# A decoder layer on one core: which pairs of a block product use seven products, and when their weight sums and snapshots are made

## The chip, the cores and the metric

The kernel runs on one core of a Trainium2 chip. The metric is device time in microseconds of one execution, given as the median of several runs. Beside the runs there is one profiled execution, from which the views of the trace come. The engines are called PE (matmul), PEld (its weight load), DVE (VectorE), ACT (ScalarE), POOL (GpSimd) and SP (SyncE, which issues the DMAs here).

## The reference

One layer over 16 meta tokens and 256 real tokens of width 2048, in float32: a normed input goes through one combined projection, a differential attention group and a gated DeltaNet group, and an output projection with residual. Then comes the part that is changed, a SwiGLU feed-forward block with a hidden width of 5632:

```python
h = h + jnp.concatenate([o_a, o_d], axis=-1) @ w_out[l]
u = rmsnorm(h, ffn_norm_w[l])
h = h + (jax.nn.silu(u @ w_gate[l]) * (u @ w_up[l])) @ w_down[l]
return h[:, LEAD:]
```

## The kernel before

**Precision.** Each float32 operand of a large product is kept as a high part in the PE's reduced format and a low part, the rest. A product is three matmuls: high × high, high × low, low × high. ACT casts the high part of a weight tile (`S.copy` in `split`, L274), the DVE subtracts it from the raw tile for the low part (L275).

**Weights.** SP loads raw tiles of 128 × 2 × 512 floats (L261) in the order in which they are used, into four slots. `split_to` makes "forms" from them, a high and a low tile each, into six buffers: the cast of a form therefore waits until the PE is done with the form six places earlier. In the FFN each block reads its weights by pairs q of two 128-row k tiles; a pair has two raw tiles (in gate and up the *gate* and the *up* tile, in down the tiles of two neighbouring column groups of 512).

**Blocks.** `block` (product line L1386 here) handles two column groups at once for 256 tokens, so that the output is four PSUM banks x (two column groups × two groups of 128 tokens). With pair q the four banks get a 2 × 2 block product: two k tiles against two column groups. A **plain pair** uses the two raw tiles as two forms and takes eight products, 24 matmuls of 128 × 512. A **seven pair** uses the scheme of seven block products: four forms, g and u (the second half only) from the raw tiles, t and s from sums of them, and 21 matmuls. Four of its products go to four side banks y of the other PSUM ring. The sums t and s take four DVE operations on halves (128 × 512): t at L292 and L293, with the u form; s at L298 and L299, with the t form. So a seven pair gives the DVE four half sums, three whole low parts and a half one; a plain pair two whole low parts.

Activations need sums too: `side_forms` (L1314 to L1333) makes them, on the DVE seven operations (one at L1320, one each at L1322 to L1325, L1331, L1332) and two casts on ACT, once for each seven pair of gate and up and of down.

**Order of the FFN.** First chunk 0 in another form (L1201), then ten chunks of `chunk`, each the gate and up columns of 512 hidden units (8 pairs), then down in two halves p = 0, 1 of 22 pairs each. In a chunk the pairs in `SEVEN` are seven pairs, in a half of down those in `DSEVEN`. After the last seven pair of a block, `mid` starts a task (`mid_task` or `down_mid`) that copies y[0] on ACT (the snapshot, L1346 in a chunk), forms sums with y[1] to y[3] on the DVE, and frees the y banks, which are the x banks of the next block. At the end of a chunk `end_task` adds (L1360, L1365, L1367 in the profile), and `to_hT` transposes the hidden activations on the PE (L1279) and splits them (L1295). Hidden chunks 8, 9 and 10 are first held in float32 and split when down begins, in `whole` (L1467); `fetch_x1` brings the residual back.

**What sets the order.** Side work is written as generators. `tasks.step()` is called after each group of products and lets waiting tasks emit instructions; `delay` is the number of steps before a task may start, `urgent` puts it first. ACT and SP run in the order in which the program emits; PE and DVE are reordered by the framework's scheduler.

Of the kernel before, what the change touches and what calls it, by code (L numbers as in the profile page):

```python
# [15 lines left out]
P = 128  # L16
# [18 lines left out]
SEVEN = (2, 5)  # L35
DSEVEN = (5, 7, 9, 11, 13, 15)
# [130 lines left out]
def layer(tc, xT, aw, x, w_in, w_ba, w_out, w_gate, w_up, w_down, cmask, dist, par, out):  # L167
# [110 lines left out]
    def split_to(n, parts=1):  # L278
        while pos[1] < min(n, len(forms)):
            m = pos[1]  # L280
            kind, i = forms[m]
            load_to(i + (1 if kind in "wg" else 2))
            src, a, b = order[i]
            if kind in "wg":
                ready[m] = split(raws[i], m, a, b, parts)
                if kind == "w":
                    raws.pop(i)
                    pos[3] += 1
            elif kind == "u":
                g, u = raws[i], raws[i + 1]  # L290
                sums_["t"] = more[0].tile([P, 2, 512], F32, tag="sum", bufs=2, name=f"t{i}")
                V.tensor_tensor(sums_["t"][:, 0], u[:, 0], g[:, 0], ALU.subtract)  # L292
                V.tensor_tensor(sums_["t"][:, 1], u[:, 1], u[:, 0], ALU.subtract)  # L293
                ready[m] = split(u, m, a, b, rows=slice(1, 2))
            elif kind == "t":
                g, u, t = raws.pop(i), raws.pop(i + 1), sums_["t"]
                sums_["s"] = s = more[0].tile([P, 2, 512], F32, tag="sum", bufs=2, name=f"s{i}")
                V.tensor_tensor(s[:, 0], u[:, 1], t[:, 0], ALU.subtract)  # L298
                V.tensor_tensor(s[:, 1], g[:, 1], s[:, 0], ALU.subtract)  # L299
                pos[3] += 2  # L300
                ready[m] = split(t, m, a, b)
            else:
                ready[m] = split(sums_["s"], m, a, b)
# [1036 lines left out]
    def mid_task(c, y, t):  # L1340

        ring = rings[(c + 1) % 2]
        for _ in range(4):
            t.append((yield from fpool[1].get(512)))
        s1, w12, u3, w22 = t
        S.copy(s1, y[0])  # L1346
# [70 lines left out]
    def chunk(c):  # L1417
# [7 lines left out]
        block(c, "u", KT // 2, SEVEN, lhs_u, None, lambda y: tasks.spawn(mid_task(c, y, t), urgent=True), end)  # L1425
# [70 lines left out]
    def down_mid(p, y):  # L1496
        yield at_least("x1n", p + 1)
        ring = rings[(NCH + p + 1) % 2]
        s1 = yield from fpool[1].get(512)
        u2 = yield from fpool[1].get(512)  # L1500
        u3 = yield from fpool[1].get(512)
        S.copy(s1, y[0])
        yield 1
# [21 lines left out]
    def down_side(i, q):  # L1525
# [12 lines left out]
        h = hT[q // 2]  # L1538
        yield from side_forms(("h", q), h[:, 0, k, :], h[:, 1, k, :], sh, sl)

    for c in range(WHOLE, NCH):
        tasks.spawn(whole(c), delay=8)
    for i, q in enumerate(DSEVEN):
        tasks.spawn(down_side(i, q), delay=4)
# [77 lines left out]
```

## Time and profile before

| what | us |
|---|---|
| median of 3 runs (lowest to highest) | 1232.11 (1231.4 to 1233.8) |
| profiled execution, its own time | 1230.78 |
| its span, first to last instruction | 1229.0 |
| ten chunks of gate and up, 553.54 to 984.20 | 430.66, PE 429.60, DVE 342.65, ACT 225.06 busy |
| from there to the end (down, output) | 244.80, PE 238.45, DVE 187.71, ACT 117.67 busy |

The busy times of the stretches come from the view of busy time by window. Busy time is a union over an engine's overlapping instructions. The DVE and the PE begin an instruction before the one ahead has ended, so the price of an instruction in a row of such is the distance of two starts, not the length. The chain of waits follows the last instruction back to what released each step; a row of it has start, length, engine, tile and line.

### The profile page before, as it was taken

What the parts mean: (1) busy time and instruction counts of PE and PEld (TensorE: products, weight loads), DVE (VectorE), ACT (ScalarE), POOL (GpSimd) and SP (SyncE); (2) the same over time, 40 slices, a digit from 0 to 9 for tenths busy, and PEclk for the clock granted to TensorE, in tenths of its full rate; (3) what the DMA queues carried; (4) which work ended last, traced back from release to release, by engine and by line L of the source; (5) the groups of instructions that cost most, each with busy time, mean ns of one, the idle gap of its engine ahead of it and who ended that gap; (6) DMA issues with size and microseconds to landing.
All of it is one profiled execution on the core that took longest, in us unless ns stands there. A gap on an engine that the chain in (4) does not pass through costs nothing.

```text
span 1229.0 us, 19155 instructions
## 1 busy us (share of the span) xinstructions
PE 1217.9 (99%) x7352; PEld 1066.9 (87%) x7352; DVE 933.4 (76%) x1487; ACT 672.3 (55%) x1059; POOL 6.0 (0%) x14
## 2 busy tenths in 40 slices
PE   9999999999999999999999999999999999999998
PEld 7999999999999988887888888888888887888887
DVE  7989974686676665667887887888788698876774
ACT  7674465375676655554555545455554555543552
POOL 0000000000000000000000000000000000000000
PEclk9999999999999999999999999999999999999999
DMA  8466553344544645675565656556465655676553
GB/s 293 124 204 196 153 180 118 118 131 147 165 136 149 219 171 178 211 265 169 182 226 160 204 189 218 192 177 229 161 201 191 205 194 182 208 247 232 199 198 117
DMA packets 151867, 228.52 MB, mean 186 GB/s; under 512 B 11736, under 2 KB 72672, under 8 KB 151264
## 3 DMA queue, kind: packets, MB, share of 16 engines
q1 hardware_dynamic: 151232, 226.78, 57.1%
q8 instruction: 57, 0.93, 0.3%
q10 hardware_dynamic: 544, 0.52, 0.1%
q14 instruction: 34, 0.28, 0.1%
HBM read 221.83 MB, written 5.45 MB: 185 GB/s over the span
## 4 chain that ended last, share of the span: by engine, by line
PE 75%; DVE 13%; DMA 6%; ACT 3%; issue 2%; SPq 0%; DVEq 0%; ACTq 0%
PE mm L1154 22%; PE mm L1386 19%; PE aux L1386 17%; PE mm L1201 10%; DVE lo L275 7%; DMA raw<-in_w_down_dram 5%; ACT hi L274 2%; PE aux L1102 1%; DVE t L292 1%; DVE s L298 1%; PE aux L1057 1%; DMA out_dram<-x 0%; DVE s L299 0%; DVE t L293 0%; DMA raw<-in_w_in_dram 0%
## 5 line engine op out<-in xcount | busy, mean ns | idle before, releaser
L275 DVE TENSOR_TENSOR lo<-raw,hi 128x1024 fp32r<-128x1024 f32 (+1 forms) x412 | 475.2, 1170 | 183.6 <-ACT hi L274 178.6
L274 ACT CAST hi<-raw 128x1024 fp32r<-128x1024 f32 (+1 forms) x412 | 410.6, 1008 | 338.9 <-PE mm L1154 92.9
L1154 PE MATMUL mm<-xh,hi 128*128 128x272 f32 (+2 forms) x896 | 258.4, 289 | 0.0
L1154 PE MATMUL mm<-xl,hi 128*128 128x272 f32 (+2 forms) x896 | 255.8, 286 | 0.6 <-DVE xl L386 0.6
L1154 PE MATMUL mm<-xh,lo 128*128 128x272 f32 (+2 forms) x896 | 254.8, 285 | 0.8 <-DVE lo L275 0.8
L1154 PEld LDWEIGHTS mm<-xh,hi 128*128 128x128 f32 x896 | 168.8, 189 | 2.1 <-issue 1.8
L1154 PEld LDWEIGHTS mm<-xl,hi 128*128 128x128 f32 x896 | 168.5, 188 | 1.6 <-DVE xl L386 1.3
L1154 PEld LDWEIGHTS mm<-xh,lo 128*128 128x128 f32 x896 | 168.2, 188 | 1.2 <-DVE lo L275 1.0
L1386 PE MATMUL mm<-hi,uh 128*128 128x512 f32 x280 | 109.4, 391 | 0.0
L1386 PE MATMUL aux<-hi,uh 128*128 128x512 f32 x280 | 109.4, 391 | 0.0
L1386 PE MATMUL aux<-hi,ul 128*128 128x512 f32 x280 | 109.0, 389 | 0.0
L1386 PE MATMUL mm<-hi,ul 128*128 128x512 f32 x280 | 109.0, 389 | 0.0
L1386 PE MATMUL aux<-lo,uh 128*128 128x512 f32 x280 | 109.0, 389 | 0.0
L1386 PE MATMUL mm<-lo,uh 128*128 128x512 f32 x280 | 109.0, 389 | 0.0
L274 ACT CAST hi<-s 128x1024 fp32r<-128x1024 f32 x32 | 33.7, 1052 | 69.4 <-DVE s L299 47.7
L1386 PE MATMUL aux<-hi,hT 128*128 128x512 f32 x208 | 68.4, 390 | 0.0
L1386 PE MATMUL mm<-hi,hT 128*128 128x512 f32 x208 | 68.1, 389 | 0.0
L1386 PEld LDWEIGHTS aux<-hi,ul 128*128 128x128 f32 x280 | 52.6, 188 | 10.9
L1386 PEld LDWEIGHTS mm<-hi,ul 128*128 128x128 f32 x280 | 52.6, 188 | 10.9
L1386 PEld LDWEIGHTS aux<-lo,uh 128*128 128x128 f32 x280 | 52.6, 188 | 10.8
L1386 PEld LDWEIGHTS mm<-hi,uh 128*128 128x128 f32 x280 | 52.6, 188 | 10.8
L1386 PEld LDWEIGHTS aux<-hi,uh 128*128 128x128 f32 x280 | 52.6, 188 | 10.7
(415 smaller groups left out, 1899.9 us busy)
## 6 DMA issues: line engine op xcount, KB each, us to landing
raw<-in_w_in_dram SPq DMA_DIRECT2D x111, 512.0 KB, 3.5
raw<-in_w_gate_dram SPq DMA_DIRECT2D x88, 512.0 KB, 4.3
raw<-in_w_up_dram SPq DMA_DIRECT2D x88, 512.0 KB, 4.5
raw<-in_w_down_dram SPq DMA_DIRECT2D x88, 512.0 KB, 4.5
raw<-in_w_out_dram SPq DMA_DIRECT2D x32, 512.0 KB, 4.3
x<-x1d SPq DMA_DIRECT2D x8, 256.0 KB, 5.4
xr<-in_xT_dram SPq DMA_DIRECT2D x7, 272.0 KB, 5.5
out_dram<-x SPq DMA_DIRECT2D x6, 256.0 KB, 5.6
```

The costliest lines, as they stand in the source:

```text
L274: S.copy(hi[:, js], raw[:, js])
L275: V.tensor_tensor(lo[:, js], raw[:, js], hi[:, js], ALU.subtract)
L292: V.tensor_tensor(sums_["t"][:, 0], u[:, 0], g[:, 0], ALU.subtract)
L298: V.tensor_tensor(s[:, 0], u[:, 1], t[:, 0], ALU.subtract)
L1057: PE.matmul(pss[m][:, cut[n]], q[ms, P * n:P * (n + 1)], k[ms, 0:NK[n]], start=True, stop=True)
L1102: PE.matmul(po[:, n, :], l, r, start=(j == 0), stop=(j == 1 + n))
L1154: PE.matmul(acc[c][:, 0:n], a[:, k, cs], b[:, kt, t0:T], start=(kt == 0 and i == 0), stop=(kt == KT - 1 and i == 2))
L1201: PE.matmul(acc[b], l, r[:, i % 2, :], start=(first and i == 0 and j == 0), stop=(last and i == len(kts) - 1 and j == 2))
L1386: PE.matmul((x if bank[0] == "x" else y)[bank[1]], l, r, start=first, stop=todo[bank] == 0)
```

## The change

`SEVEN` goes from two pairs (2 and 5) to three (2, 4 and 6) of eight, `DSEVEN` from six pairs (5, 7 to 15) to seven (7, 9 to 19) of 22. In `split_to` both sums of weights, t and s, are made in the step of the form g, the pair's first; both raw tiles are let go with u. The snapshot is emitted in `mid` at once, as soon as the tiles for it are free, and the task for the rest starts without delay. The tasks `whole`, `down_side` and `fetch_x1(0)` start after 24 steps instead of 8, 4 and 16, and `down_side` waits for the split of its own hidden chunk.

```diff
@@ -32,8 +32,8 @@
 WR, WS = 4, 4
 WS2 = 2
 WHOLE = 8
-SEVEN = (2, 5)
-DSEVEN = (5, 7, 9, 11, 13, 15)
+SEVEN = (2, 4, 6)
+DSEVEN = (7, 9, 11, 13, 15, 17, 19)
 PER_STEP = 2
 SLOT = 4
 WARM = 14
@@ -279,28 +279,26 @@
         while pos[1] < min(n, len(forms)):
             m = pos[1]
             kind, i = forms[m]
-            load_to(i + (1 if kind in "wg" else 2))
+            load_to(i + (1 if kind == "w" else 2))
             src, a, b = order[i]
-            if kind in "wg":
-                ready[m] = split(raws[i], m, a, b, parts)
-                if kind == "w":
-                    raws.pop(i)
-                    pos[3] += 1
-            elif kind == "u":
+            if kind == "w":
+                ready[m] = split(raws.pop(i), m, a, b, parts)
+                pos[3] += 1
+            elif kind == "g":
                 g, u = raws[i], raws[i + 1]
-                sums_["t"] = more[0].tile([P, 2, 512], F32, tag="sum", bufs=2, name=f"t{i}")
-                V.tensor_tensor(sums_["t"][:, 0], u[:, 0], g[:, 0], ALU.subtract)
-                V.tensor_tensor(sums_["t"][:, 1], u[:, 1], u[:, 0], ALU.subtract)
-                ready[m] = split(u, m, a, b, rows=slice(1, 2))
-            elif kind == "t":
-                g, u, t = raws.pop(i), raws.pop(i + 1), sums_["t"]
-                sums_["s"] = s = more[0].tile([P, 2, 512], F32, tag="sum", bufs=2, name=f"s{i}")
+                ready[m] = split(g, m, a, b)
+                t, s = (more[0].tile([P, 2, 512], F32, tag="sum", bufs=2, name=f"{n}{i}") for n in "ts")
+                V.tensor_tensor(t[:, 0], u[:, 0], g[:, 0], ALU.subtract)
+                V.tensor_tensor(t[:, 1], u[:, 1], u[:, 0], ALU.subtract)
                 V.tensor_tensor(s[:, 0], u[:, 1], t[:, 0], ALU.subtract)
                 V.tensor_tensor(s[:, 1], g[:, 1], s[:, 0], ALU.subtract)
+                sums_["t"], sums_["s"] = t, s
+            elif kind == "u":
+                raws.pop(i)
+                ready[m] = split(raws.pop(i + 1), m, a, b, rows=slice(1, 2))
                 pos[3] += 2
-                ready[m] = split(t, m, a, b)
             else:
-                ready[m] = split(sums_["s"], m, a, b)
+                ready[m] = split(sums_[kind], m, a, b)
             pos[1] += 1
 
     def next_w():
@@ -1340,10 +1338,7 @@
     def mid_task(c, y, t):
 
         ring = rings[(c + 1) % 2]
-        for _ in range(4):
-            t.append((yield from fpool[1].get(512)))
         s1, w12, u3, w22 = t
-        S.copy(s1, y[0])
         yield 1
         V.tensor_tensor(w12, y[1], s1, ALU.add)
         V.tensor_tensor(u3, y[2], w12, ALU.add)
@@ -1422,7 +1417,13 @@
                 for b in range(2):
                     tasks.spawn(end_task(c, b, x, t), urgent=True)
 
-        block(c, "u", KT // 2, SEVEN, lhs_u, None, lambda y: tasks.spawn(mid_task(c, y, t), urgent=True), end)
+        def mid(y):
+            tasks.until(lambda: fpool[1].live == 0)
+            t.extend(fpool[1].now((512,)) for _ in range(4))
+            S.copy(t[0], y[0])
+            tasks.spawn(mid_task(c, y, t), delay=0, urgent=True)
+
+        block(c, "u", KT // 2, SEVEN, lhs_u, None, mid, end)
         mark(f"up{c}")
 
     def keep_x1():
@@ -1493,14 +1494,9 @@
     def need_h(kt):
         return at_least(f"hT{kt // 4}", 2 if kt // 4 < WHOLE else 3)
 
-    def down_mid(p, y):
+    def down_mid(p, y, s1, u2, u3):
         yield at_least("x1n", p + 1)
         ring = rings[(NCH + p + 1) % 2]
-        s1 = yield from fpool[1].get(512)
-        u2 = yield from fpool[1].get(512)
-        u3 = yield from fpool[1].get(512)
-        S.copy(s1, y[0])
-        yield 1
         V.tensor_tensor(u2, y[1], s1, ALU.add)
         V.tensor_tensor(u3, y[2], u2, ALU.add)
         for b, c, t in ((0, 1, y[3]), (1, 1, y[3]), (0, 1, u2), (1, 1, u3), (0, 0, s1), (1, 0, u3)):
@@ -1535,21 +1531,28 @@
                 t = rest[:, o:o + 6 * P]
             sh, sl = (t[:, 3 * P * j:3 * P * (j + 1)].rearrange("p (a b) -> p a b", b=P) for j in range(2))
         k = slice(2 * q % 4, 2 * q % 4 + 2)
-        h = hT[q // 2]
-        yield from side_forms(("h", q), h[:, 0, k, :], h[:, 1, k, :], sh, sl)
+        c = q // 2
+        yield at_least(f"hT{c}", 2 if c < WHOLE else 3)
+        h, l = (hT[c][:, 0], hT[c][:, 1]) if c < WHOLE else hT[c]
+        yield from side_forms(("h", q), h[:, k, :], l[:, k, :], sh, sl)
 
     for c in range(WHOLE, NCH):
-        tasks.spawn(whole(c), delay=8)
+        tasks.spawn(whole(c), delay=24)
     for i, q in enumerate(DSEVEN):
-        tasks.spawn(down_side(i, q), delay=4)
-    tasks.spawn(fetch_x1(0), delay=16)
+        tasks.spawn(down_side(i, q), delay=24)
+    tasks.spawn(fetch_x1(0), delay=24)
     for p in range(2):
         def end(col, x):
             for b in range(2):
                 tasks.spawn(down_end(p, b, col, x[2 * col + b]), urgent=True)
 
-        block(NCH + p, "h", FFN // P // 2, DSEVEN, lhs_h, need_h,
-              lambda y: tasks.spawn(down_mid(p, y), urgent=True), end)
+        def mid(y):
+            tasks.until(lambda: fpool[1].live <= 1)
+            t = [fpool[1].now((512,)) for _ in range(3)]
+            S.copy(t[0], y[0])
+            tasks.spawn(down_mid(p, y, *t), delay=0, urgent=True)
+
+        block(NCH + p, "h", FFN // P // 2, DSEVEN, lhs_h, need_h, mid, end)
         if p == 0:
             tasks.spawn(fetch_x1(1), delay=12)
     tasks.until(lambda: not tasks.list)
```

What the scheduler makes of it is seen in the order of the engines. Place one is the DVE in a steady chunk of gate and up, around a seven pair. Names: `raw` is a loaded tile, `hi` and `lo` a form's parts, `t` and `s` the sums. Before:

```order
L275 TENSOR_TENSOR lo_7593<-raw_7548,hi_7592 128x1024
L275 TENSOR_TENSOR lo_7605<-raw_7575,hi_7604 128x1024
L292 TENSOR_TENSOR t_7614<-raw_7587,raw_7575 128x512
L293 TENSOR_TENSOR t_7614<-raw_7587 128x512
L275 TENSOR_TENSOR lo_7618<-raw_7587,hi_7617 128x512
L298 TENSOR_TENSOR s_7633<-raw_7587,t_7614 128x512
L299 TENSOR_TENSOR s_7633<-raw_7575,s_7633 128x512
L275 TENSOR_TENSOR lo_7637<-t_7614,hi_7636 128x1024
L275 TENSOR_TENSOR lo_7657<-s_7633,hi_7656 128x1024
```

and with the change (pair 4 of a chunk; L291 to L294 are the lines of the four half sums now, and the rows ahead of this piece are two L1293 rows, three whole low parts, one L1362 row and the half low part of the *up* tile of pair 2):

```order
L291 TENSOR_TENSOR t_7622<-raw_7583,raw_7519 128x512
L275 TENSOR_TENSOR lo_7607<-raw_7517,hi_7606 128x1024
L292 TENSOR_TENSOR t_7622<-raw_7583 128x512
L275 TENSOR_TENSOR lo_7619<-raw_7519,hi_7618 128x1024
L293 TENSOR_TENSOR s_7623<-raw_7583,t_7622 128x512
L275 TENSOR_TENSOR lo_7632<-raw_7583,hi_7631 128x512
L294 TENSOR_TENSOR s_7623<-raw_7519,s_7623 128x512
L275 TENSOR_TENSOR lo_7646<-t_7622,hi_7645 128x1024
L275 TENSOR_TENSOR lo_7656<-s_7623,hi_7655 128x1024
L275 TENSOR_TENSOR lo_7672<-raw_7610,hi_7671 128x1024
```

The first half of t has moved ahead of the low part of the *up* tile of the plain pair before it and the low part of this pair's own *gate* tile; the halves of s lie between low parts. Pair 6 follows in the same way; pair 2 has its four halves ahead of the additions that end the chunk before.

Place two is the DVE in the first half of down, one plain and one seven pair, late in the run of seven pairs. Before:

```order
L275 TENSOR_TENSOR lo_10642<-raw_10597,hi_10641 128x1024
L275 TENSOR_TENSOR lo_10654<-raw_10599,hi_10653 128x1024
L292 TENSOR_TENSOR t_10660<-raw_10627,raw_10599 128x512
L293 TENSOR_TENSOR t_10660<-raw_10627 128x512
L275 TENSOR_TENSOR lo_10664<-raw_10627,hi_10663 128x512
L298 TENSOR_TENSOR s_10673<-raw_10627,t_10660 128x512
L275 TENSOR_TENSOR lo_10677<-t_10660,hi_10676 128x1024
L299 TENSOR_TENSOR s_10673<-raw_10599,s_10673 128x512
L275 TENSOR_TENSOR lo_10691<-s_10673,hi_10690 128x1024
```

and with the change:

```order
L291 TENSOR_TENSOR t_11197<-raw_11167,raw_11129 128x512
L292 TENSOR_TENSOR t_11197<-raw_11167 128x512
L293 TENSOR_TENSOR s_11198<-raw_11167,t_11197 128x512
L275 TENSOR_TENSOR lo_11182<-raw_11127,hi_11181 128x1024
L294 TENSOR_TENSOR s_11198<-raw_11129,s_11198 128x512
L275 TENSOR_TENSOR lo_11194<-raw_11129,hi_11193 128x1024
L275 TENSOR_TENSOR lo_11207<-raw_11167,hi_11206 128x512
L275 TENSOR_TENSOR lo_11221<-t_11197,hi_11220 128x1024
L275 TENSOR_TENSOR lo_11231<-s_11198,hi_11230 128x1024
```

The sums of the seven pair now lead, ahead of the low part of the second tile of the plain pair before; before, they followed the pair's own first tile. In the second half of down the order was of this kind already.

On PE the block's products fall from 2880 rows to 2844; the DVE's rows rise from 1415 to 1503, ACT's from 894 to 922, SP's stay at 442. In the first of the ten chunks the PE's order has the transposes of chunk 0 after 12 of its products before, and after 21 and 23 now. Everything ahead of the sums of activations for the first chunk is in the same order.

## The prediction

> **What bounds the kernel now.** I read the page's busy shares first, then busy time by stretches of the span, then the waits of the PE, then the chain of waits and the DVE's timeline where they point.
>
> ```profile
> PE 1217.9 (99%) x7352; PEld 1066.9 (87%) x7352; DVE 933.4 (76%) x1487; ACT 672.3 (55%) x1059; POOL 6.0 (0%) x14
> ```
>
> ```profile
> 739.68:825.80 86.12, 86.12 (x390) 71.50 (x389) 69.50 (x81) 45.14 (x51) 0.00 (x0) 1.00 0.61 196
> ...
> 990.00:1000.00 10.00, 10.00 (x50) 8.36 (x49) 9.93 (x20) 5.45 (x8) 0.00 (x0) 1.00 0.62 209
> 1000.00:1010.00 10.00, 10.00 (x46) 8.29 (x45) 10.00 (x21) 6.66 (x13) 0.00 (x0) 1.00 0.44 144
> 1010.00:1020.00 10.00, 9.33 (x42) 7.39 (x40) 10.00 (x23) 4.55 (x8) 0.00 (x0) 1.00 0.33 119
> 1020.00:1030.00 10.00, 8.93 (x37) 6.54 (x36) 8.83 (x11) 5.57 (x6) 0.00 (x0) 1.00 0.62 211
> ...
> 1180.00:1190.00 10.00, 9.62 (x43) 7.61 (x42) 8.54 (x10) 5.78 (x6) 0.00 (x0) 1.00 0.51 161
> ```
>
> The columns are PE, PEld, DVE, ACT, POOL busy, granted clock, DMA share, GB/s. The first stretch is two chunks of gate and up, 43.06 us each: the PE never pauses, the DVE has 34.75 of 43.06 us filled, ACT 22.6, and the DMA engines 0.61. The PE falls short only where the down product begins (42 and 37 matmuls in 1010 to 1030 us where an undisturbed stretch has 46: 13 short) and a little at 1180. In 990 to 1020 the DVE has no free time: that shortage is the DVE's. The clock is 1.00 throughout.
>
> ```profile
> PE mm L1386 <- DVE lo L275: 1.8, 3, 0.8
> ...
> PE mm L1279 <- DVE gact L1308: 1.1, 1, 1.1
> ```
>
> These are the PE's stalls in the FFN that the waits name: three on the low parts of weights, and one in front of the transposes of the first chunk. So a removed matmul comes off the end as long as the DVE keeps up, and the question is where it doesn't.
>
> **What it removes: 36 matmuls.** The order has 2880 products at the block's product line before and 2844 after: three in each of ten chunks, three in each half of down. Their price is the spacing in an undisturbed run, from the chain of waits:
>
> ```profile
> 961.85 11.56 PE mm L1386 x51
> ```
>
> 11.56 / 51 = 0.2267 us; 36 of them are 8.16 us, of which 6.80 in the chunks and 1.36 in down. A chunk would take 43.06 − 0.68 = 42.38 us.
>
> The Trainium skill ("TensorE: Matmul & The Clock Gate", section "Back-to-back issue gap") gives a sustained 131 ns for a matmul of 512 columns; by it 36 would be worth an estimated 4.7 us. The trace disagrees with 227 ns at a granted clock of 1.00, and the measurement decides.
>
> **What it adds on the DVE.** Durations overlap there, so I cost by start to start:
>
> ```profile
> 792.01 0.69 DVE L292 TENSOR_TENSOR t<-raw,raw 128x512 f32<-128x512 f32 x1 [0.50 <-DMA raw<-in_w_up_dram]
> 792.62 0.68 DVE L293 TENSOR_TENSOR t<-raw 128x512 f32<-128x512 f32 x1
> 793.22 0.69 DVE L275 TENSOR_TENSOR lo<-raw,hi 128x512 fp32r<-128x512 f32 x1
> ...
> 796.85 1.23 DVE L275 TENSOR_TENSOR lo<-s,hi 128x1024 fp32r<-128x1024 f32 x1 [0.48 <-ACT hi L274]
> ...
> 1023.23 3.49 DVE L275 TENSOR_TENSOR lo<-raw,hi 128x1024 fp32r<-128x1024 f32 x3
> 1026.63 0.69 DVE L292 TENSOR_TENSOR t<-raw,raw 128x512 f32<-128x512 f32 x1
> ```
>
> A half (128x512) takes 0.605 us, a full low part 3.40 / 3 = 1.13 us. A plain pair has two full low parts; a seven pair three full ones, a half one and four half sums. Each further seven pair costs the DVE 1.13 + 5 × 0.605 = 4.16 us. ACT gets four casts for two:
>
> ```profile
> L274 ACT CAST hi<-s 128x1024 fp32r<-128x1024 f32 x32 | 33.7, 1052 | 69.4 <-DVE s L299 47.7
> ```
>
> at most 2 × 1.05 = 2.1 us, 24.7 of 42.4: no bound. The loads are the same 442 rows on SP.
>
> **Ten chunks: the cover.** The DVE gets 34.75 + 4.16 = 38.9 us of work for 42.38, so 3.5 us are left for its waits. The new order puts the t sum of pairs 4 and 6, which needs the *up* tile of its pair, ahead of the low part of the *up* tile before it; if that load is late, the low parts behind it are late too. Only down's second half shows what such a place costs:
>
> ```profile
> 1147.40 0.69 DVE L292 TENSOR_TENSOR t<-raw,raw 128x512 f32<-128x512 f32 x1 [1.92 <-DMA raw<-in_w_down_dram]
> ...
> 1158.34 0.69 DVE L292 TENSOR_TENSOR t<-raw,raw 128x512 f32<-128x512 f32 x1 [2.16 <-DMA raw<-in_w_down_dram]
> ...
> 1170.10 0.69 DVE L292 TENSOR_TENSOR t<-raw,raw 128x512 f32<-128x512 f32 x1 [2.98 <-DMA raw<-in_w_down_dram]
> ...
> 1181.45 0.69 DVE L292 TENSOR_TENSOR t<-raw,raw 128x512 f32<-128x512 f32 x1 [2.58 <-DMA raw<-in_w_down_dram]
> ```
>
> ```profile
> 1152.80 5.42 DMA raw<-in_w_down_dram
> ...
> 1163.74 6.24 DMA raw<-in_w_down_dram
> ...
> 1175.50 5.84 DMA raw<-in_w_down_dram
> ```
>
> There the load of a pair's second tile (in a chunk the *up* tile) starts when the slot of the second tile two pairs back is let go, at its low part, and takes 5.4 to 6.2 us. In the new chunk order there lie after that release, for pair 6, a half sum and three full low parts (0.6 + 3.4 = 4.0 us): a wait of 1.4 to 2.2. For pair 4 there lie six instructions, three of them of 128x512 (two at L1293, one at L1362), 3 × 0.605 + 3.4 = 5.2 us: a wait of 0.2 to 1.0. I take the middles, 1.8 and 0.6: the DVE's own cycle is 41.3 us, 1.1 below the PE's. The cushion in front of it, from the same chunk:
>
> ```profile
> 801.81 1.36 PE mm L1386 x6
> 803.17 2.04 PE aux L1386 x9
> ```
>
> In pair 5 the last of the nine products into aux use the s form, from 803.17 + 6 × 0.2267 = 804.5; its low part was done at 796.85 + 1.23 = 798.1. That is 6.4 us of lead, so a wait of 2.2 in one place isn't felt. I take 0 for the chunks; if the cover goes, they pay as in the slower rival.
>
> **First chunk.**
>
> ```profile
> 560.60 0.68 DVE gact L1308
> ...
> 561.32 0.66 PE mm L1279 x4
> ```
>
> The transposes at L1279 stalled 1.1 us for the DVE. In the PE's order they stood 12 matmuls into the chunk and now stand 21 and 23, 2.0 to 2.5 us later; but a third set of activation sums (2.07 us, below) goes ahead on the DVE. The stall may vanish (−1.2) or grow (+0.9); I take −0.3.
>
> **Head of down.** Six sets of sums of activations and three whole casts fall into the stretch before the first seven pair. One set is
>
> ```profile
> 1012.81 0.68 DVE L1320 TENSOR_TENSOR gact<-hT 128x512 f32<-128x512 f32 x1
> 1013.41 0.28 DVE L1331 TENSOR_TENSOR hT<-gact,hT 128x128 fp32r<-128x128 f32 x1
> 1013.61 0.28 DVE L1322 TENSOR_TENSOR gact<-gact 128x128 f32<-128x128 f32 x1
> 1013.81 0.28 DVE L1324 TENSOR_TENSOR gact<-gact 128x128 f32<-128x128 f32 x1
> ...
> 1014.22 0.55 DVE L1332 TENSOR_TENSOR rest<-gact,rest 128x384 fp32r<-128x384 f32 x1
> 1014.69 0.28 DVE L1325 TENSOR_TENSOR gact<-gact,gact 128x128 f32<-128x128 f32 x1
> ```
>
> 0.60 + 5 × 0.20 + 0.47 = 2.07 us. The first seven pair moves from 5 to 7: the PE has two plain pairs more, 48 × 0.2267 = 10.9 us, and the DVE in them four low parts (4.5) and one more set (2.07): 6.6. That frees 4.3 us, more than the 13 × 0.2267 = 2.9 us that the PE lost there. Sums and whole casts are also spawned to come later (24 steps). Bounds: all of it goes (−2.9), or none, if the late sums gather in front of pair 7. I take −2.3.
>
> **Seven pairs of down, first half.** Before, this loop (one seven, one plain pair) had 10.07 us on the DVE, 1.20 of it a wait for ACT:
>
> ```profile
> 1032.15 1.23 DVE L275 TENSOR_TENSOR lo<-s,hi 128x1024 fp32r<-128x1024 f32 x1 [1.20 <-ACT hi L274]
> ...
> 1036.70 0.68 DVE L292 TENSOR_TENSOR t<-raw,raw 128x512 f32<-128x512 f32 x1
> ```
>
> (1026.63 to 1036.70), for 45 × 0.2267 = 10.20 on the PE: just enough. With s made at once with g that wait goes, and the loops at pairs 9 and 11 need 5 × 1.13 + 5 × 0.605 = 8.7 us, which gains 1.5 each. From pair 13 on the order has t ahead of the plain pair's low parts, as in the second half, at up to 11.35 (next part): 0.55 to 1.15 too much, three or four times, 1.7 to 4.6 together, against 3.0 gained. Bounds 0 and +1.6; I take +0.5.
>
> **Second half.** The starts 1147.40 to 1181.45 are three loops, 11.35 us each, against 10.20: each eats 1.15 us of lead, until the PE stalls at 1180. The order of these loops is unchanged and there is one more of them, so +1.15 once more, bounds 0.7 and 1.8.
>
> **Snapshot.** The copy out of y[0] is the same instruction, one cast earlier on ACT. Five casts lie between the last s cast and it; six buffers per form mean that the fifth already needs the PE past the t form, and y[0] ended in the g form before: no wait, 0. The casts behind it have the buffers' lead as cover; a late one would cost its 1.05. With pair 19 the last, the sums of the middle come 48 matmuls (10.9 us) before a half's end instead of 144; they are eight halves (4.8 us) beside eight low parts at most, already ahead. The tail stays:
>
> ```profile
> 1224.13 1.10 DVE x L1520 x3
> ```
>
> **The sum**, against the profiled execution (1230.78 us; span 1229.0): −8.16 − 0.3 − 2.3 + 0.5 + 1.15 = −9.1, so 1221.7. The median of the runs is 1.33 higher, 1232.11, so **1223.0 us**.
>
> **Rivals.**
> *Slower: the DVE becomes the bound in the chunks.* If all three seven pairs of a chunk wait for their load as in the second half, mean (1.92 + 2.16 + 2.98 + 2.58) / 4 = 2.41 us, a cycle is 38.9 + 7.2 = 46.1 against 43.06 now: 3.1 × 10 less the lead of 6.4 is +24, and with down at −2.0 (−1.36 − 2.3 + 0.5 + 1.15) about 1254 us. It bites once waits pass 3.5 us in a chunk and makes the kernel slower past about 5 (4.2 to fill 43.06, 0.6 for a tenth of the lead and 0.2 for a tenth of what down gives). For it: the two sums moved forward, and the waits for ACT that two chunks have now, 11.5 us:
>
> ```profile
> L275 DVE TENSOR_TENSOR lo<-raw,hi 128x1024 fp32r<-128x1024 f32 x28 | 33.5, 1222 | 12.0 <-ACT hi L274 11.5
> ```
>
> Against: the lead of 6.4 us in the same chunks shows those waits to be slack, and the releases counted above give 2.4 us of waits, not 7.2. 6%.
> The Trainium skill ("VectorE: DVE Perf Modes", section "The DRAIN you can't avoid") has the next operation start only when the pipe is empty; by it the five halves and one full would cost an estimated 4.67, 0.5 more in a chunk, which favours this rival. The section after it lets an operation that isn't held start sooner, and the trace agrees with that: 0.605 start to start at a length of 0.69.
> *Down keeps its stall or gives more back.* The sums gather at pair 7 (stall of 2.9 stays), or both halves pay their upper bounds (+1.6, +1.8): 1223.0 + 2.3 = 1225.3, to 1223.0 + 2.3 + 1.1 + 0.65 + 1.2 (first chunk) = 1228.3. For it: the order still has rows of the last two sets between the t sum of pair 7 and its low parts. 17%.
> *All is hidden.* No stall at the first chunk or at the head, lower bounds in the halves: 1232.11 − 8.16 − 1.2 − 2.9 + 0.7 = 1220.5. 7%.
> That it does not do what it says is ruled out by the 36 fewer rows.
>
> **How the numbers follow.** My forecast has 70%. Range 1219.5 to 1228: the hidden case less a microsecond, up to down's bounds; the slower rival and the far end of down's lie outside. A difference under 0.2% (2.46 us) can't be told from none: faster is below 1229.65. The forecast and the hidden case are faster, down's rival nearly always (10 of 17%): 0.87; within 0.07; slower 0.06.
>
> **What would show it.** Chunks of 42.38 us with the PE full and the DVE near 39; waits for the up load of about 2 us at pair 6's t sum; 45 or 46 matmuls in each 10 us around the first seven pair of down; starts of L291 11.3 us apart in the second half, and a stall before its end of up to 1.8 us in all. PE waits on L275 inside chunks would make the forecast wrong.

## The result and the profile after

The changed kernel takes 1224.22 us in the median (1223.92 to 1225.47, four runs) against 1232.95 us for the kernel before, measured beside it (1231.4 to 1234.7). The ratio is 0.9926, 95% interval 0.9908 to 0.9945: 8.7 us, or 0.7%, faster, between 6.8 and 11.3 us. The two profiled executions lie nearer together, 1230.78 and 1224.38 us by their own times (spans of 1229.0 and 1222.6): that of the kernel before was shorter than any of its four runs. The DVE has 86 rows more in the profile (1573, against 1487 before).

The page of the kernel after, its first part, and busy time by stretches (columns PE, PEld, DVE, ACT, POOL, granted clock, DMA share, GB/s). The first stretch is two chunks.

```profile
PE 1209.2 (99%) x7316; PEld 1060.0 (87%) x7316; DVE 983.6 (80%) x1573; ACT 692.3 (57%) x1087; POOL 6.1 (0%) x14
```

```profile
653.38:738.14 84.76, 84.76 (x383) 70.34 (x383) 77.32 (x93) 48.40 (x55) 0.00 (x0) 1.00 0.61 199
...
1010.00:1020.00 10.00, 10.00 (x46) 8.27 (x45) 10.00 (x26) 3.10 (x6) 0.00 (x0) 1.00 0.52 178
1020.00:1030.00 10.00, 10.00 (x46) 8.28 (x45) 9.74 (x17) 6.66 (x10) 0.00 (x0) 1.00 0.51 163
...
1170.00:1180.00 10.00, 9.47 (x42) 7.46 (x42) 6.92 (x10) 6.12 (x7) 0.00 (x0) 1.00 0.47 155
1180.00:1190.00 10.00, 9.07 (x40) 7.21 (x39) 7.30 (x10) 5.15 (x6) 0.00 (x0) 1.00 0.54 186
1190.00:1200.00 10.00, 8.21 (x37) 6.46 (x36) 6.49 (x8) 4.07 (x5) 0.00 (x0) 1.00 0.54 177
```

A chunk takes 84.76 / 2 = 42.38 us with the PE full and the DVE at 38.7. At the head of down the PE now makes 46 matmuls in each 10 us. In the second half of down it lacks 4 + 6 + 9 = 19 of them, where before it lacked 3.

The waits of the PE in the kernel after:

```profile
PE mm L1381 <- DVE lo L275: 3.3, 3, 1.8
PE mm L1277 <- DVE gact L1306: 1.3, 1, 1.3
```

The first row is the second half of down, the second the transposes of the first chunk. The DVE's timeline of the second half shows where the first comes from:

```profile
1173.09 0.69 DVE L291 TENSOR_TENSOR t<-raw,raw 128x512 f32<-128x512 f32 x1 [3.08 <-DMA raw<-in_w_down_dram]
...
1184.55 0.69 DVE L291 TENSOR_TENSOR t<-raw,raw 128x512 f32<-128x512 f32 x1 [2.69 <-DMA raw<-in_w_down_dram]
...
1196.84 0.69 DVE L291 TENSOR_TENSOR t<-raw,raw 128x512 f32<-128x512 f32 x1 [3.51 <-DMA raw<-in_w_down_dram]
```

The loops are 11.46 and 12.29 us long, for 10.20 us of work on the PE. The tail is as before:

```profile
1217.73 1.10 DVE x L1516 x3
```

To compare kernels by stage I took from each trace the start of the first block product, of the first one of each half of down, and of the last. All in us; "front" is everything ahead of the ten chunks, "tail" what comes after the last product's start. The spans are those of single profiled executions, so a ratio, which goes by all runs, can differ from what a span suggests.

```
                 span    front  ten chunks  chunks 2-10, each  half 1  half 2  tail
before          1229.0  556.9     432.0          43.07         119.4   116.1   4.6
after           1222.6  557.8     425.4          42.39         115.8   118.9   4.6
shift_only      1233.5  558.8     430.9          43.07         121.9   117.3   4.6
only_chunks     1221.7  557.8     424.6          42.39         119.1   115.8   4.6
six_down        1221.3  560.0     424.7          42.39         116.5   115.6   4.6
old_delays      1226.6  560.1     425.0          42.39         117.4   119.6   4.6
pin_down        1225.8  558.7     425.0          42.39         122.9   114.7   4.6
pin_half        1220.5  559.3     426.1          42.51         115.8   114.7   4.6
seven_only      1244.4  557.8     441.3          44.19         122.0   118.8   4.6
old_sums        1233.1  557.4     432.5          43.22         116.4   122.3   4.6
old_snap        1226.8  557.7     430.6          43.09         116.3   117.7   4.6
extra1          1224.8  558.4     427.6          42.67         116.4   117.9   4.6
extra2          1241.3  557.8     442.6          44.33         119.3   116.6   5.1
best3           1219.4  560.4     423.9          42.39         115.8   114.7   4.6
```

From before to after: front +0.9, ten chunks −6.5, first half of down −3.6, second half +2.8, sum −6.4.

### The profile page after: what moved, and what is told of

It is laid out like the page before. It is cut to its first block, busy times and chain, and to the rows that moved or that the text cites. A ratio compares the mean times of both kernels' runs of the same rounds, so it can differ in the third digit from the quotient of the medians.

```text
span 1222.6 us, 19223 instructions
## 1 busy us (share of the span) xinstructions
PE 1209.2 (99%) x7316; PEld 1060.0 (87%) x7316; DVE 983.6 (80%) x1573; ACT 692.3 (57%) x1087; POOL 6.1 (0%) x14
## 4 chain that ended last, share of the span: by engine, by line
PE 85%; DVE 7%; DMA 4%; ACT 2%; issue 1%; SPq 0%; DVEq 0%; ACTq 0%
PE aux L1381 25%; PE mm L1152 23%; PE mm L1381 21%; PE mm L1199 10%; DVE lo L275 3%; DMA raw<-in_w_down_dram 3%; ACT hi L274 1%; PE aux L1100 1%; PE aux L1055 1%; DMA raw<-in_w_in_dram 0%; PE mm L1277 0%; DVE s L293 0%; DMA raw<-in_w_up_dram 0%; DVE r L581 0%; PE aux L1277 0%
## 5 line engine op out<-in xcount | busy, mean ns | idle before, releaser
L274 ACT CAST hi<-raw 128x1024 fp32r<-128x1024 f32 (+1 forms) x412 | 405.1, 996 | 325.0 <-PE mm L1152 93.3
L1381 PE MATMUL aux<-hi,uh 128*128 128x512 f32 x260 | 101.6, 391 | 0.0
L1381 PE MATMUL mm<-hi,uh 128*128 128x512 f32 x260 | 101.6, 391 | 0.0
L1381 PE MATMUL aux<-hi,ul 128*128 128x512 f32 x260 | 101.3, 390 | 0.0
L1381 PE MATMUL mm<-hi,ul 128*128 128x512 f32 x260 | 101.2, 389 | 0.0
L1381 PE MATMUL aux<-lo,uh 128*128 128x512 f32 x260 | 101.2, 389 | 0.0
L1381 PE MATMUL mm<-lo,uh 128*128 128x512 f32 x260 | 101.2, 389 | 0.0
L274 ACT CAST hi<-s 128x1024 fp32r<-128x1024 f32 x44 | 46.3, 1053 | 38.0 <-DVE s L294 34.5
L291 DVE TENSOR_TENSOR t<-raw,raw 128x512 f32<-128x512 f32 x44 | 30.2, 687 | 38.7 <-DMA raw<-in_w_down_dram 25.2
L274 ACT CAST hi<-t 128x1024 fp32r<-128x1024 f32 x44 | 46.3, 1053 | 26.2 <-DVE t L292 11.3
```

The costliest lines, as they stand in the source:

```text
L274: S.copy(hi[:, js], raw[:, js])
L291: V.tensor_tensor(t[:, 0], u[:, 0], g[:, 0], ALU.subtract)
L1381: PE.matmul((x if bank[0] == "x" else y)[bank[1]], l, r, start=first, stop=todo[bank] == 0)
```

## The experiments

The theory behind the prediction was: the PE sets the time; the stall at the head of down is the DVE's shortage of time ahead of the first seven pair; the loss in the second half of down is a load that the hoisted t sum waits for; the chunks have cover, and the places of the sums and of the snapshot cost nothing. The rivals: the delays removed the stall; the second half is short of load slots or of lead; the chunks have no cover.

### The head of down

**Moving the seven pairs of the kernel before.**

```diff
-DSEVEN = (5, 7, 9, 11, 13, 15)
+DSEVEN = (7, 9, 11, 13, 15, 17)
```

(and each set of sums waits for the split of its own hidden chunk)

> The kernel before with its six seven pairs of down moved from 5, 7 to 15 to 7, 9 to 17 (and each set of activation sums of down waiting for the split of its own hidden chunk, as pair 17 needs); nothing else. Theory: the stall of 2.84 us at the head of down goes because the PE has 10.9 us more there, span 1229.0 - 2.8 = 1226.2, and up to 1.5 more if the second half stalls longer. Rival: the stall hangs on when the sums are emitted, which is as before: span 1229.

Measured: ratio 1.0019 (1.0007 to 1.0030), span 1233.5: no gain. The view by stretches and the waits say why:

```profile
1010.00:1030.00 20.00, 20.00 (x90) 16.36 (x89) 15.97 (x28) 9.40 (x13) 0.00 (x0) 1.00 0.55 187
```

```profile
PE aux L1386 <- DVE lo L275: 4.0, 4, 1.2
PE mm L1386 <- DVE lo L275: 1.6, 1, 1.6
```

The stall at the head is gone, as the theory has it. But the scheduler chose another order for the DVE in the first half too, the one with t ahead, and its loops grew from 10.05 us to between 11.15 and 11.64:

```profile
1044.99 0.69 DVE L292 TENSOR_TENSOR t<-raw,raw 128x512 f32<-128x512 f32 x1 [2.22 <-DMA raw<-in_w_down_dram]
...
1056.63 0.69 DVE L292 TENSOR_TENSOR t<-raw,raw 128x512 f32<-128x512 f32 x1 [2.71 <-DMA raw<-in_w_down_dram]
...
1068.22 0.69 DVE L292 TENSOR_TENSOR t<-raw,raw 128x512 f32<-128x512 f32 x1 [2.82 <-DMA raw<-in_w_down_dram]
```

Four waits of 1.0 us in the mean follow in the first half (the row of 4.0 above). Neither span that was expected came out; the step on the head held, and the price of the order was seen for the first time outside the second half.

**Down's pairs of before in the changed kernel.**

```diff
-DSEVEN = (7, 9, 11, 13, 15, 17, 19)
+DSEVEN = (5, 7, 9, 11, 13, 15)
```

> The changed kernel with down's seven pairs as before (six, from pair 5): gate and up have three seven pairs, sums, snapshot and delays as changed. Its span is compared with 1222.6 us of the changed kernel. Theory: down gets six matmuls back (+1.36), the PE loses time again in front of the first seven pair because the DVE has two plain pairs less to make its sums in (+2 to +3), and the second half has one loop of its late kind fewer (-2.1 to -3.4): span 1222 to 1225. Rival: the later start of the sums (24 steps) is what took the stall at the head away: then 46 matmuls in each 10 us there still, span 1220.5 to 1222.

Measured: span 1221.7, ratio 0.9953 (0.9937 to 0.9970). The profiled execution took 1223.49 us, the median of the six runs is 1227.18; the span would fit the rival too, so the waits decide. The stall is back, for all that the delays are in:

```profile
PE aux L1381 <- DVE lo L275: 1.0, 1, 1.0
PE aux L1381 <- ACT hi L274: 0.9, 1, 0.9
```

and the stalls of the second half are down to one of 0.3 us. The first half takes 119.1 us, 2.5 more than without a stall (116.5 with as many matmuls in the run without the seventh seven pair, below). So the delays alone do not remove the stall at the head.

**The delays of before in the changed kernel.**

```diff
-        tasks.spawn(whole(c), delay=24)
+        tasks.spawn(whole(c), delay=8)
-        tasks.spawn(down_side(i, q), delay=24)
+        tasks.spawn(down_side(i, q), delay=4)
-    tasks.spawn(fetch_x1(0), delay=24)
+    tasks.spawn(fetch_x1(0), delay=16)
```

> The changed kernel with the delays of the tasks of down as before (8, 4 and 16 steps instead of 24). Theory: the stall at the head of down hangs on the two plain pairs more, not on the delays: span 1222.6 within 1, at most 0.5 us of stall in 1000 to 1030. Rival: with early sums the additions that end the last chunk come late and the stall is back: 1 to 3 us there, span 1224 to 1226.

Measured: span 1226.6, ratio 0.9955 (0.9940 to 0.9971), 39 matmuls in 1010 to 1020 where an undisturbed stretch has 46:

```profile
1010.00:1020.00 10.00, 9.05 (x39) 6.96 (x38) 9.61 (x21) 6.20 (x9) 0.00 (x0) 1.00 0.45 151
```

About 1.5 us of the stall came back (7 matmuls of 0.2267 us): the rival was right here. In the changed kernel both edits are needed, the two pairs and the later sums; in the kernel before, the two pairs alone did it.

### The second half of down

**Without the seventh seven pair.**

```diff
-DSEVEN = (7, 9, 11, 13, 15, 17, 19)
+DSEVEN = (7, 9, 11, 13, 15, 17)
```

> The changed kernel without its last seven pair in down (7, 9 to 17). Theory: the second half's last loop, whose stall was 2.06 us, goes with it, for 6 matmuls more on the PE (+1.36): span 1222.6 - 0.7 = 1221.9, so the seventh pair is worth less than nothing; stalls in the second half 1.9 us. Rival: the stall belongs to the half as such (a lead that is short from its start) and not to each loop: span 1222.6 + 1.36 = 1224.

Measured: span 1221.3, ratio 0.9916 (0.9899 to 0.9933). The second half takes 115.6 us instead of 118.9, and its stalls are 0.1 us in place of 4.0. That is more than one loop's 2.1. The starts of the t sums account for the rest. In the changed kernel the last four loops are 11.13, 11.86, 11.47 and 12.29 us, 5.95 over four times 10.20; a lead of 1.95 us stood ahead of the first (the low part was ready that long before its use), and 5.95 − 1.95 = 4.0 is the stall. Here the loops are 11.35, 11.30 and 11.18, 3.2 over, and the lead was 3.2. Each loop eats 0.9 to 2.1 us, the lead pays for the first ones, and what is left is the stall. The seventh pair saves 1.36 us of matmuls in the two halves together, and the stalls of the second half are 4.0 us with it and 0.1 without. By the ratios the two kernels can't be told apart (0.9916 and 0.9926).

**The DVE in the program's order from the start of down.** `manual_schedule` keeps the named engines in the order of the program; ACT and SP are named already.

```diff
+    cm_order.__exit__(None, None, None)
+    cm_order = tc.manual_schedule(engines=PINNED | {ET.DVE})
+    cm_order.__enter__()
     for p in range(2):
```

> The changed kernel with the DVE, too, in the order of the program from the start of down on: in the second half the four half sums of a seven pair then follow the low parts of the plain pair before and of its own first tile, instead of standing ahead of them. The same instructions and loads. Theory: the low parts behind a sum that waits for its load are what the PE waits for; now five full low parts (5.7 us) lie between the release of the load's slot and the sum, for a load of 5.4 to 6.8, so a wait of at most 1.1 in a loop of 8.7 + 1.1 = 9.8 us, under the PE's 10.2: stalls of the second half 0 to 0.5 instead of 4.0, span 1218.6 to 1219.2. Rival: four load slots are too few for this pattern in any order: stalls of 2.5 or more remain, span 1221 or more.

Measured: span 1225.8, ratio 0.9952 (0.9938 to 0.9966). The second half does what the theory says, 114.7 us without a stall, loops of 10.20, and the t sums there wait for no load at all. But the head of down, which the expectation left out, pays for it, since the sums of activations stand in the program's order there too:

```profile
PE aux L1381 <- ACT hi L274: 4.0, 1, 4.0
```

**The same in the second half alone.**

```diff
+        if p == 1:
+            cm_order.__exit__(None, None, None)
+            cm_order = tc.manual_schedule(engines=PINNED | {ET.DVE})
+            cm_order.__enter__()
         block(NCH + p, "h", FFN // P // 2, DSEVEN, lhs_h, need_h, mid, end)
```

> The changed kernel with the DVE in the order of the program in the second half of down alone; all rows ahead of it as in the changed kernel. Theory: the stalls of the second half (0.80, 1.20 and 2.06 us) go, as they went in the run that pinned all of down, and nothing else moves: span 1222.6 - 4.0 = 1218.6, within 0.9 for what the stretch ahead of the feed-forward part varies. Rival: the stalls went there because the 6 us lost at the head of down left the loads that much ahead: then 2 us or more of stalls stay, span 1220.6 or more.

Measured: ratio 0.9896 (0.9874 to 0.9918), median 1220.91 us; span 1220.5, with a front 1.5 us longer than in the changed kernel and 0.7 us more in the ten chunks, whose rows are in the same order; the second half is 114.7 us, 4.2 less. (The 95% interval of the ratio still overlaps that of the changed kernel, 0.9908 to 0.9945; the stage is what shows the gain.) The DVE's timeline:

```profile
1173.74 0.68 DVE L291 TENSOR_TENSOR t<-raw,raw 128x512 f32<-128x512 f32 x1
...
1181.43 2.58 DVE L275 TENSOR_TENSOR lo<-raw,hi 128x1024 fp32r<-128x1024 f32 x2 [1.07 <-ACT hi L274]
1183.94 0.68 DVE L291 TENSOR_TENSOR t<-raw,raw 128x512 f32<-128x512 f32 x1
```

Two low parts now stand ahead of t, which no longer waits for its load; the loop is 10.20 us, the PE's. The same instructions and loads, with the rows of PE and ACT in the same order as in the changed kernel and those of the DVE in another from the second half on: the four slots were enough, and the order was the cause.

### The chunks

**Three seven pairs in the kernel before, nothing else.**

```diff
-SEVEN = (2, 5)
+SEVEN = (2, 4, 6)
```

> The kernel before with three seven pairs (2, 4, 6) in gate and up, nothing else. Theory: the thirty matmuls come off whole, since the DVE has cover with the sums at either place: chunks of 42.38 us, span 1229.0 - 6.8 = 1222.2, plus or minus 1.5 for the stalls at the first chunk and at the head of down. Rival: only with the sums made at the pair's first tile does a third seven pair fit: chunks of 43 us or more, span 1227 or more.

Measured: ratio 1.0097 (1.0078 to 1.0116), span 1244.4: slower than before, with thirty matmuls fewer; the rival's bound of 43 us holds. The chunks take 44.19 us. What the PE waits for is not the weights' low parts:

```profile
PE aux L1386 <- DVE gact L1351: 3.4, 5, 0.8
...
PE mm L1386 <- DVE gact L1351: 2.4, 4, 0.8
...
PE aux L1386 <- DVE gact L1348: 1.5, 4, 0.4
```

L1348 to L1351 are the sums behind the snapshot. They read the side banks, which are the next chunk's x banks, and the next chunk waits at its first products. ACT's timeline at such a turn from one chunk to the next (the next chunk's first product starts at 777.33):

```profile
773.55 1.05 ACT L274 CAST hi<-raw 128x1024 fp32r<-128x1024 f32 x1 [2.71 <-DMA raw<-in_w_gate_dram]
775.74 1.05 ACT L274 CAST hi<-raw 128x1024 fp32r<-128x1024 f32 x1 [1.15 <-DMA raw<-in_w_up_dram]
776.70 0.58 ACT L1346 COPY gact<-mm 128x512 f32<-128x512 f32 x1
```

The copy stands behind two casts that wait 2.71 and 1.15 us for their loads, and ACT runs in order. In the changed kernel it stands one cast earlier and is done 4.6 us before the turn (at 771.33):

```profile
765.22 1.05 ACT L274 CAST hi<-raw 128x1024 fp32r<-128x1024 f32 x1 [0.48 <-DMA raw<-in_w_gate_dram]
766.17 0.58 ACT L1423 COPY gact<-mm 128x512 f32<-128x512 f32 x1
767.30 1.05 ACT L274 CAST hi<-raw 128x1024 fp32r<-128x1024 f32 x1 [0.55 <-DMA raw<-in_w_up_dram]
```

The next two runs undo one of the two edits each.

**The snapshot of before in the changed kernel.** `mid_task` and `down_mid` get their tiles and the copy back:

```diff
-            S.copy(t[0], y[0])
-            tasks.spawn(mid_task(c, y, t), delay=0, urgent=True)
+            tasks.spawn(mid_task(c, y, t), urgent=True)
```

> The changed kernel with the snapshot and the tasks behind it as before (copy emitted by the task, one step later and after the tiles are waited for, in chunks and in down). Theory, from the run of the three seven pairs alone, where the next chunk's first products waited for L1346 and L1348 to L1351: the late snapshot and its sums hold the side banks that the next chunk needs, 1 to 1.5 us a chunk: span 1222.6 + 10 to 15, 1232 to 1238. Rival: those stalls came from the sums of weights at their old places crowding the DVE, and the snapshot's place is worth nothing (0, as the prediction costed it): 1222 to 1224.

Measured: ratio 0.9991 (0.9976 to 1.0005), span 1226.8 (the profiled execution took 1228.63 us, the median of the ten runs is 1232.38). Chunks of 43.09 us, 0.70 more each, so the ten matmul triples bring nothing:

```profile
PE mm L1277 <- DVE gact L1365: 2.3, 4, 0.6
...
PE aux L1384 <- DVE gact L1349: 1.8, 4, 0.8
```

The edit is worth something, as the theory of this run had it, but by the chunks of the profile about half of what was expected; the waits are at the next chunk's banks (L1349) and at the transposes behind the last additions (L1365). Here, too, the copy stands behind a cast that waits for a load; the next chunk starts at 773.81:

```profile
769.97 1.05 ACT L274 CAST hi<-raw 128x1024 fp32r<-128x1024 f32 x1 [0.83 <-DMA raw<-in_w_up_dram]
770.93 0.58 ACT L1344 COPY gact<-mm 128x512 f32<-128x512 f32 x1
```

Over the ten chunks the copy is done 1.8 us before the turn in the mean (4.8 in the changed kernel), and the last sum behind it 3.5 us after the turn (0.1 before it); the bank that this sum lets go is needed 15 products, or 3.4 us, after the turn. So 3.0 of the 3.6 us by which the sums come later are the copy's. The rest is not separated: the PE's order is the same, but the scheduler chose another for the DVE in the chunks.

**The sums of weights of before in the changed kernel.** t is made with u again, s with t.

```diff
-                t, s = (more[0].tile([P, 2, 512], F32, tag="sum", bufs=2, name=f"{n}{i}") for n in "ts")
...
+                V.tensor_tensor(s[:, 0], u[:, 1], t[:, 0], ALU.subtract)
+                V.tensor_tensor(s[:, 1], g[:, 1], s[:, 0], ALU.subtract)
+                pos[3] += 2
+                ready[m] = split(t, m, a, b)
```

> The changed kernel with the sums of weights at their old places (t with u, s with t). Theory: neither place is waited for by the PE in gate and up, and the second half of down keeps the order with the sums ahead: span 1222.6 within 1. Rival: the sums at the first tile bought the cover in the chunks: 1225 or more; or they caused the longer second half: stalls there 0.7 or less, span 1219.5.

Measured: ratio 1.0005 (0.9991 to 1.0020), span 1233.1. The first rival was nearer: chunks of 43.22 us. The waits are those of the transposes:

```profile
PE mm L1279 <- DVE gact L1364: 3.4, 3, 1.2
PE aux L1279 <- DVE gact L1364: 1.9, 2, 1.1
```

The second half of down, 122.3 us, did not get shorter with the sums at their old places.

**More work for the DVE.** The first half of t made again, once or twice, in each seven pair of gate and up; the repeats serve no purpose.

```diff
-                V.tensor_tensor(t[:, 0], u[:, 0], g[:, 0], ALU.subtract)
+                for _ in range(3 if i < DOWN else 1):
+                    V.tensor_tensor(t[:, 0], u[:, 0], g[:, 0], ALU.subtract)
```

(three for extra2, two for extra1)

> The changed kernel with the first half sum of t made three times in each seven pair of gate and up (twice to no use): 6 x 0.605 = 3.6 us more for the DVE in a chunk, 38.6 + 3.6 = 42.2 of 42.38. Theory: the DVE's waits in the chunks are slack but for about 0.8 us for the load of pair 6, so its cycle comes to 43.0, 0.6 over the PE's: ten chunks cost 6 less the lead of 3, span 1222.6 + 3 = 1226 (1222.6 to 1229). Rival, the slower case of the prediction: the waits are not slack (7 us a chunk), and all of 3.6 us a chunk is paid: span 1250 or more.

> The changed kernel with one needless half sum in each seven pair of gate and up: 3 x 0.605 = 1.8 us more for the DVE in a chunk. Theory: there is a free lead to be used up first; with 3.6 us a chunk about 1.5 us a chunk were paid, so 2.1 were free and 1.8 cost next to nothing: span 1222.6 to 1224. Rival: no free lead, a constant share (1.5 of 3.6) of every added microsecond is paid: 7.6 us, span 1230.

Measured: extra2 1.0077 (1.0057 to 1.0097), span 1241.3, chunks of 44.33 us: of 3.63 us added 1.94 are paid. extra1 0.9962 (0.9949 to 0.9975), span 1224.8, chunks of 42.67: of 1.8 added 0.28 are paid. So there is a free lead, of 1.5 to 1.7 us in a chunk if all beyond it is paid; extra2 lay between its two cases, and a fixed share is out. The scheduler moved other rows of the DVE too, and in extra2 some of the PE, so the size of the lead is rough. Where the lead ends first is again the turn of the chunk; in extra1

```profile
PE mm L1279 <- DVE gact L1364: 0.9, 3, 0.5
```

and in extra2

```profile
PE mm L1279 <- DVE gact L1364: 2.2, 3, 0.8
PE aux L1279 <- DVE gact L1364: 1.9, 4, 0.7
```

In the trace of before the additions that end a chunk were done 2.6 to 5.4 us ahead of their transposes, in the trace of after 1.05 to 3.8. So thin a lead can run out in the changed order itself: in the run with the second half pinned, whose chunks have the rows of the changed kernel, one chunk took 43.50 us, with a wait of 0.6 us for the additions ahead of its transposes.

### A version that beats both

The second half in the program's order, and the transposes of chunk 0 later (`ffn_task`):

```diff
-        yield 2
+        yield 9
         yield from to_hT(c, b, g_)
```

> The changed kernel with the DVE in the order of the program in the second half of down, and the transposes of chunk 0 seven steps later, behind 33 products of the first chunk instead of 21 and 23 (7.5 us in instead of 4.8). Theory: the stall of the first chunk (1.1 to 1.5 us: the last additions of chunk 0 are done 7.1 us in) goes too: from first to last product 656.6 - 1.1 = 655.5 us, span about 1219. Rival: the later transposes free their banks too late for the first seven pair, which then waits as long: 656.5 or more.

Measured: median 1220.17 us (1218.54 to 1221.26), ratio 0.9896 (0.9880 to 0.9913); span 1219.4. From the first product to the last it takes 654.4 us against 660.2 in the changed kernel, and no wait on a line of the blocks or of their transposes is left in the view of waits. The first chunk takes 42.40 us like the others. By the ratio nothing is gained over the second half's order alone (0.9896 both). The front was 2.6 us longer than in the profile of the changed kernel, with its rows in the same order (below), so the span shows less than the stages do.

## Why the prediction was right, and where not

The median was forecast at 1223.0 and came at 1224.2; by stage the sum was less good, and that the medians came so near is partly luck (the end of this part).

- **36 matmuls at 0.2267 us** held. Chunks 2 to 10 take 42.39 us (42.38 forecast). The DVE's 38.9 in a chunk was measured as 38.7. The wait of pair 4's t for its load, put at 0.6, was 0; that of pair 6's, put at 1.8, was 1.1 in the mean of the ten chunks (0.1 to 2.2), for one

```profile
751.56 0.69 DVE L291 TENSOR_TENSOR t<-raw,raw 128x512 f32<-128x512 f32 x1 [0.79 <-DMA raw<-in_w_up_dram]
```

- **The cover in the chunks** held in its result and not in its reason, so that the chunks came out as forecast was luck. The prediction measured the lead at the s form of pair 5 (6.4 us). The chain that runs short first is the turn of the chunk: snapshot, sums, x banks of the next chunk, and last additions, transposes. Its lead is 1.05 us in the worst place, not 6.4. The slower rival named the right engine and the wrong place: the DVE has room for some 1.6 us more, and past that the PE waits at the turn, not at the low parts behind a late load.
- **The snapshot at 0, and the sums' places**, which the prediction weighed as a risk and then put at 0, are the steps that failed without being seen, since their edits were in. Undone, they cost 0.70 and 0.83 us a chunk, each the whole of what three matmuls save; with neither of them three seven pairs make the kernel slower (1.0097). "Five casts lie between" was right, but the prediction asked only whether the copy waits for the PE, and not what the casts ahead of it on ACT wait for.
- **The first chunk** was put at −0.3; the PE's gap there went from 1.2 to 1.5 us.
- **The head of down**, −2.3: the whole 2.8 went. The two pairs and the later sums were both needed.
- **The first half's loops**, +0.5: none of it was paid. The t sums there start 8.4 to 10.8 us apart after the first loop, and the late ones stay within the lead.
- **The second half**, +1.15 with bounds to 1.8: the term that was mis-sized. Its stalls grew by 3.4 us, from 0.66 to 4.0. One loop more was counted, at the mean of before; but the three loops that were there before grew (11.13, 11.86 and 11.47 us for 10.94, 11.76 and 11.36), the new one took 12.29 (11.69 in the mean of four, not 11.35), and the lead ahead of them was 1.95 us, not 2.96. Why that lead shrank was not tried. The mechanism, a load that the hoisted t waits for, is shown by the run that changes the order there and nothing else.
- **The front** was taken as equal and was 0.9 us longer.

So in the profiles an underestimated loss (+2.3 in the second half) and the front (+0.9) stand against a head that gave 0.5 more and the 0.5 that the first half did not take, with 0.6 more lost at the first chunk: −9.1 became −6.4. The medians of the runs, at −8.7, lie nearer to the forecast than the two profiles, because the profiled execution of the kernel before lies below its runs; how much of that is the front, which varies by more than the difference (below), was not separated.

## What to carry to other kernels

When matmuls are taken from a kernel whose second engine has some 10% of slack, look for the chain with the least lead at the turn between blocks, where banks change hands, and not only at the steady loop: here a copy one place further back on an in-order engine, behind a cast that waits for a load, cost as much as the three matmuls saved (0.70 us a chunk, with the order that the scheduler then gave the DVE). Where a scheduler sets an engine's order, the same edit can flip a loop into an order that waits for a load; read the order of every loop the edit touches, and pin it where it has gone wrong (in one half of down that alone gave 4 us). A lead that is eaten loop by loop hides a loss until the loop count grows: work out period minus period, times the number of loops, against the lead at the start.

## What the runs showed of the hardware that was not expected

After some pauses the PE ran slower for a while, with no wait in between. In the run with the DVE in the program's order from the start of down, about 5.4 us were lost at the head, with one wait of 4.0; the stretches around it:

```profile
1010.00:1020.00 10.00, 10.00 (x46) 8.29 (x45) 9.79 (x27) 3.97 (x9) 0.00 (x0) 1.00 0.62 203
1020.00:1030.00 10.00, 5.28 (x21) 3.54 (x20) 9.72 (x24) 4.26 (x8) 0.00 (x0) 0.97 0.19 61
1030.00:1040.00 10.00, 10.00 (x39) 7.93 (x39) 9.96 (x12) 6.92 (x8) 0.00 (x0) 0.86 0.54 176
```

The granted clock was 0.86 in 1030 to 1040, where the PE was busy throughout and made 39 matmuls in place of 46: 1.6 us on top of the pause. It also happened with a shorter pause of 2.0 us in the run with the sums at their old places, where four us had

```profile
1198.00:1202.00 4.00, 3.98 (x10) 3.12 (x11) 4.00 (x5) 2.00 (x2) 0.00 (x0) 0.57 0.50 153
```

and after a wait of 2.0 us in the attention part of the fastest version:

```profile
155.50:158.90 3.40, 3.40 (x18) 3.40 (x17) 3.40 (x12) 1.80 (x10) 0.00 (x0) 0.50 0.90 260
```

Taken as narrowly, the first two have a granted clock of 0.50 as well (1029.4 to 1032.7 and 1198.3 to 1201.7): about 3.4 us at half the clock each time, and 1.00 again behind it. But a pause as long as the second in the changed kernel (1.95 us at 1197.75) left the clock at 1.00. The Trainium skill ("TensorE: Matmul & The Clock Gate", section "Part 1: The HAM clock gate (the "warmup" mystery)") says that the clock halves after an idle window of about 3.4 us; the first case, with its wait of 4.0 us, agrees with it. The other two do not: their pauses were shorter, and the clock halved all the same. No run here shows what set it off.

The front, whose rows stand in the same order, took between 556.9 and 560.4 us in the fourteen profiles. In the four longest (559.3 to 560.4) most of the extra time comes in one place of the attention part, 152 to 158 us in; in the fastest version there is a wait of the PE that the changed kernel does not have:

```profile
PE aux L730 <- DVE r L709: 2.0, 1, 2.0
```

An earlier row of that line on the DVE waits 2.60 us for its load there, against 0.62 in the changed kernel, and the DVE's rows behind it come 2.1 us later:

```profile
147.15 0.36 DVE L709 TENSOR_SCALAR r<-r,par_sb 128x144 f32<-128x144 f32 x1 [2.60 <-DMA r<-e]
```

The half clock of the row at 155.50 follows that wait and adds about a microsecond: matmuls in it start 0.22 us apart, and 0.12 behind it. What made the load late was not tried. The variation of the front is as large as several of the terms above, which is why the stages were compared and not the spans alone.
